# Modulation weight loads taken in pairs on four column tiles of 512 columns, with VectorE adding the partial sums

## The chip, the cores and the metric

The kernel runs on one core of one Trainium2 chip. Times are device microseconds (us) of that core from launch to end; three executions of the kernel before took 1745.45, 1746.52 and 1747.11 us, median 1746.52 us. The profile shows one further execution of the same program, taken by the hardware profiler.

## The reference

One step of one decoder layer for 256 prompt tokens and 8 sample tokens (264 columns), in float32. What matters here is the modulation: nine conditioning vectors (one for the prompt, eight for the samples) pass through a silu and a 2048 x 6144 weight matrix and give shift, scale and gate.

```python
def trunk_layer(x, c, prm, conv_prefix, h0, attend):
    mod = jax.nn.silu(c) @ prm['w_mod'] + prm['b_mod']
    shift, scale, gate = jnp.split(mod[:, None, :], 3, axis=-1)
    h = rmsnorm(x, prm['g_pre']) * (1 + scale) + shift
    (u_a, v_a, z_a, x_b, z_b, q, k, v, q_i, k_i, w_i, z_c, g_m) = split_proj(h @ prm['w_in'])
    ...
    merged = g[:, :, 0] * p_a + g[:, :, 1] * p_b + g[:, :, 2] * p_c
    o = merged @ prm['w_out']
    x = x + gate * rmsnorm(o, prm['g_post'])
```

## The kernel before

Activations stand with features on partitions and the 264 tokens along the free axis. A feature tile is 128 columns of a projection: 16 blocks of 128 x 128 weights, each multiplied three times (high by high, high by low, low by high part of a float32 split in two), so 48 matmuls of 264 columns for a tile. Weights come in **units** of eight blocks, 512 KB each, one DMA on SyncE's queue per unit; ScalarE makes the high part `wh` (line 302) and VectorE the low part `wl` (line 306), each in two halves of 512 columns, one to three units ahead of the product.

The modulation weights `w_mod` come over the same queue and into the same buffers (`raw`, six of them, and four extra `rawx` until the last load of shift and scale), again 512 KB for each load. They aren't split: `mod_item` (line 397) multiplies them in plain float32, with the nine vectors (`cpad`, padded to 32 columns) as the stationary operand, so that each matmul takes a tile of 128 rows by 32 columns of TensorE and four such column tiles can work at a time. `w_mod` is cut into pieces (`PIECES`, line 48): shift and scale of 1, 1, 2, 4, 4 and 4 blocks of features, then the gate in two halves. Pieces 0 and 1 have 4 loads each (four k each), piece 2 has 8 (two k each), pieces 3 to 5 and the two gate halves 16 each (one k of 1024 columns): 96 loads. In a load, `groups_of` gives each column tile its own quarter of the columns (128 or 256 of them, two tiles alone in pieces 0 and 1), and PSUM sums over k.

`_stream` (line 75) writes down the order in which loads are issued and used. The first 32 tiles (`EARLY`) are computed in parts of K: with the first piece of h they do one block each, and so on, while the next piece's modulation loads are put between their units; partial products are collected in SBUF (`part`, lines 1014 to 1022) by VectorE, in the first part by ScalarE too. The gate's 32 loads are put one behind each unit of the tiles `u` and `za`, in the middle of the kernel. TensorE works strictly in this order, so a modulation load stands between the matmuls of two units.

When a piece's last load has been used, `mod_piece` (line 450) copies the sums from PSUM (`ms`, line 440, on ScalarE), turns them by TensorE transposes (`modT`, line 434), adds the bias on VectorE and makes h's high and low parts `hh` and `hl`, which the next parts of the early tiles wait for. `mod_gate` (line 477) does the first half of that for the gate. The work of a piece is spread over the following products by `Tasks`.

## Time and profile before

| what | value |
|---|---|
| time, median of three executions | 1746.52 us |
| profiled execution: first to last instruction (span) | 1614.2 us |
| outside the span, by the median | 132.3 us |
| TensorE busy | 1578.5 us, 98% |
| VectorE busy | 990.1 us, 61% |
| ScalarE busy | 807.9 us, 50% |
| mean granted TensorE clock | 0.990 of full speed |
| data moved | 326.26 MB, mean 202 GB/s |

The trace holds the span alone; of the profiled execution's time outside it, nothing is recorded, so the 132.3 us are the difference to the median of the other three executions. A matmul in the trace is shown with its start and a modelled end: neighbours overlap, and the pace of TensorE is read from one start to the next. A float32 matmul leaves two records, so a load of 1024 columns with four matmuls shows as x8.

### The profile page before, as it was taken

What the parts mean: (1) busy time and instruction counts of PE and PEld (TensorE: products, weight loads), DVE (VectorE), ACT (ScalarE), POOL (GpSimd) and SP (SyncE); (2) the same over time, 40 slices, a digit from 0 to 9 for tenths busy, and PEclk for the clock granted to TensorE, in tenths of its full rate; (3) what the DMA queues carried; (4) which work ended last, traced back from release to release, by engine and by line L of the source; (5) the groups of instructions that cost most, each with busy time, mean ns of one, the idle gap of its engine ahead of it and who ended that gap; (6) DMA issues with size and microseconds to landing.
All of it is one profiled execution on the core that took longest, in us unless ns stands there. A gap on an engine that the chain in (4) does not pass through costs nothing.

```text
span 1614.2 us, 33342 instructions
## 1 busy us (share of the span) xinstructions
PE 1578.5 (98%) x13289; PEld 1518.1 (94%) x13289; DVE 990.1 (61%) x2111; ACT 807.9 (50%) x1628; POOL 295.5 (18%) x411
## 2 busy tenths in 40 slices
PE   8999999998889999999999999999999999999998
PEld 7888899998879999998889999999999999999997
DVE  6876589754446645544546654444777777766654
ACT  5333368554435444443334444444777777754442
POOL 4000256577730001000000000000211111100011
PEclk9999999999989999999999999999999999999999
DMA  8898863655445555657885556555465545555652
GB/s 337 304 362 286 284 207 119 192 180 155 156 151 174 185 182 184 201 184 268 286 273 186 172 182 235 181 181 181 152 198 174 173 162 186 180 190 183 234 183 83
DMA packets 91867, 326.26 MB, mean 202 GB/s; under 512 B 12320, under 2 KB 12768, under 8 KB 91328
## 3 DMA queue, kind: packets, MB, share of 16 engines
q1 hardware_dynamic: 86608, 313.18, 57.4%
q0 software_dynamic: 5104, 10.96, 2.3%
q8 instruction: 104, 1.70, 0.4%
q14 instruction: 51, 0.42, 0.1%
HBM read 320.35 MB, written 3.67 MB: 201 GB/s over the span
## 4 chain that ended last, share of the span: by engine, by line
PE 70%; DVE 1%; issue 0%; POOL 0%; DMA 0%; ACT 0%; DVEq 0%; ACTq 0%
PE acc L1010 68%; PE pmod L407 1%; PE spP L838 0%; PE giP L879 0%; PE gaP L879 0%; POOL gv L716 0%; DVE x L161 0%; DVE ls L158 0%; DMA gv<-in_cv,rows 0%; DVE ls L981 0%; DVE wl L160 0%; PE rsP L1063 0%; DVE o L158 0%; DVEq L1154 0%; ACT wh L157 0%
## 5 line engine op out<-in xcount | busy, mean ns | idle before, releaser
L160 DVE TENSOR_TENSOR wl<-raw,wh 128x512 fp32r<-128x512 f32 x926 | 613.2, 706 | 371.9 <-ACT wh L157 352.8
L1010 PE MATMUL acc<-hh,wh 128*128 128x264 f32 x2832 | 822.5, 290 | 6.8 <-DVE part L159 2.6
L1010 PE MATMUL acc<-hh,wl 128*128 128x264 f32 x2832 | 805.1, 284 | 1.9 <-DVE wl L160 1.9
L1010 PE MATMUL acc<-hl,wh 128*128 128x264 f32 x2832 | 806.0, 285 | 0.1
L157 ACT ACTIVATE wh<-raw 128x512 fp32r<-128x512 f32 x926 | 530.3, 622 | 496.6 <-PE acc L1010 357.4
L1010 PEld LDWEIGHTS acc<-hh,wh 128*128 128x128 f32 x2832 | 536.6, 189 | 41.0 <-issue 25.1
L1010 PEld LDWEIGHTS acc<-hl,wh 128*128 128x128 f32 x2832 | 537.0, 190 | 0.7 <-DVE hl L160 0.4
L1010 PEld LDWEIGHTS acc<-hh,wl 128*128 128x128 f32 x2832 | 534.2, 189 | 2.3 <-DVE wl L160 2.3
L1010 PE MATMUL acc<-ah,wh 128*128 128x264 f32 x768 | 217.9, 284 | 0.0
L1010 PE MATMUL acc<-al,wh 128*128 128x264 f32 x768 | 217.6, 283 | 0.0
L1010 PE MATMUL acc<-ah,wl 128*128 128x264 f32 x768 | 217.4, 283 | 0.0
L1010 PEld LDWEIGHTS acc<-al,wh 128*128 128x128 f32 x768 | 144.7, 188 | 0.0
L1010 PEld LDWEIGHTS acc<-ah,wh 128*128 128x128 f32 x768 | 144.6, 188 | 0.0
L1010 PEld LDWEIGHTS acc<-ah,wl 128*128 128x128 f32 x768 | 144.0, 187 | 0.0
L810 POOL TENSOR_TENSOR mg<-mg,gp 128x264 f32<-128x264 f32 x16 | 12.0, 752 | 473.8 <-DVE gp L161 473.8
L159 DVE TENSOR_TENSOR part<-acc,part 128x264 f32<-128x264 f32 x128 | 51.6, 428 | 35.6 <-PE acc L1010 35.2
L1010 PE MATMUL acc<-mh,wh 128*128 128x264 f32 x256 | 72.6, 284 | 0.0
L1010 PE MATMUL acc<-ml,wh 128*128 128x264 f32 x256 | 72.5, 283 | 0.0
L1010 PE MATMUL acc<-mh,wl 128*128 128x264 f32 x256 | 72.5, 283 | 0.0
L716 POOL DMA_INDIRECT gk<-in_ck,rows x64 | 64.2, 1003 | 19.4 <-issue 16.3
L716 POOL DMA_INDIRECT gv<-in_cv,rows x64 | 62.1, 970 | 19.5 <-issue 18.3
L1010 PEld LDWEIGHTS acc<-ml,wh 128*128 128x128 f32 x256 | 48.2, 188 | 0.0
(377 smaller groups left out, 1266.8 us busy)
## 6 DMA issues: line engine op xcount, KB each, us to landing
raw<-in_wall SPq DMA_DIRECT2D x463, 512.0 KB, 3.7
raw<-in_wmod SPq DMA_DIRECT2D x73, 512.0 KB, 5.6
rawx<-in_wmod SPq DMA_DIRECT2D x23, 512.0 KB, 6.4
rawx<-in_wall SPq DMA_DIRECT2D x19, 512.0 KB, 6.0
xr<-in_xT SPq DMA_DIRECT2D x4, 528.0 KB, 5.6
wrg<-in_wrg SPq DMA_DIRECT2D x1, 2048.0 KB, 8.5
x<-in_xp SPq DMA_DIRECT2D x1, 2048.0 KB, 9.5
out_yp<-x SPq DMA_DIRECT2D x8, 256.0 KB, 2.4
```

The lines of the kernel that those rows point to most:

```text
L157: copy = lambda out, x, scale=1.0: act.activation(out, x, AF.Copy, scale=scale)
L159: add = lambda out, x, y: dve.tensor_tensor(out, x, y, OP.add)
L160: sub = lambda out, x, y: dve.tensor_tensor(out, x, y, OP.subtract)
L407: pe.matmul(MOD[q][32 * g:32 * g + 32, 0:n], cpad[:, k, :], r[:, c:c + n], start=k == 0, stop=k == KB - 1, skip_group_check=True)
L716: pool.indirect_dma_start(out=to, out_offset=None, in_=a["ck" if what == "gk" else "cv"], in_offset=bass.IndirectOffsetOnAxis(ap=rows[:, n ...
L810: pool.tensor_tensor(S["mg"][:, j, :], S["mg"][:, j, :], x, OP.add)
L1010: pe.matmul(c[:, 0:T], x[:, kk * P:(kk + 1) * P], y[:, k, :], start=n == 0 and (kk == 0 if early else k == 0), stop=n == 2 and (kk == nk - ...
```

## The change

The 96 loads stay as they are, in size and content. What changes:

- `_stream` puts them in twos: two loads in a row, then units. The gate's pairs stand behind each whole tile (two units) and no longer one behind each unit.
- `mod_item` does nothing at a pair's first load and works off both at the second. The work of both is one list of (k, up to 512 columns), and entry x goes to column tile x mod 4. So a column tile no longer owns a part of the columns; it sums the k that fall to it, over 512 columns (256 in pieces 0 and 1).
- The copy out of PSUM takes two instructions where there are 512 columns, the first 256 columns on ScalarE, the others on VectorE; there are n / 128 transposes, and `tensor_reduce` on VectorE adds the partial sums over the column tiles into `mr`, from which the bias is added.

```diff
 def _stream():
             while done < len(ms) and done * MOD_BY <= j * len(ms):
-                items.append(ms[done])
-                done += 1
+                items += ms[done:done + 2]
+                done += 2
...
             items.append(("w", n, [(j, k0, 8)]))
             n += 1
-            if gate and ORDER[j][0] in ("u", "za"):
-                items.append(gate.pop(0))
+        if gate and ORDER[j][0] in ("u", "za"):
+            items += gate[:2]
+            del gate[:2]
...
-    def groups_of(q):
+    def shape_of(q):
         width = MODS[q][0][0]
-        groups = min(4, width // P)
-        return groups, width // groups
+        return width, min(512, width), max(1, width // 512)

     def mod_item(i):
         _, q, m = items[i]
-        width, ks, _ = MODS[q][m]
-        groups, n = groups_of(q)
-        if m == 0:
+        if m % 2 == 0:
+            return
+        width, n, halves = shape_of(q)
+        if m == 1:
             MOD[q] = pst("pmod")
-        r = used(i)
-        for x, k in enumerate(ks):
-            for g in range(groups):
-                c = x * width + g * n
-                pe.matmul(MOD[q][32 * g:32 * g + 32, 0:n], cpad[:, k, :], r[:, c:c + n],
-                          start=k == 0, stop=k == KB - 1, skip_group_check=True)
+        work = []
+        for x in (i - 1, i):
+            ks = MODS[q][items[x][2]][1]
+            r = used(x)
+            work += [(k, r[:, c * width + h * n:c * width + (h + 1) * n])
+                     for c, k in enumerate(ks) for h in range(halves)]
+        for x, (k, r) in enumerate(work):
+            g = x % 4
+            pe.matmul(MOD[q][32 * g:32 * g + 32, 0:n], cpad[:, k, :], r, start=m == 1 and x < 4,
+                      stop=m == len(MODS[q]) - 1 and x >= len(work) - 4, skip_group_check=True)
...
+    def mod_rows(q):
+        n = shape_of(q)[1]
+        p = MOD.pop(q)
+        ms = []
+        for c in range(0, n, 256):
+            ms.append(w("ms"))
+            (dve.tensor_copy if c else copy)(ms[-1][:, 0:256], p[:, c:c + 256])
+        return ms
+
     def mod_turn(q, ms):
-        groups, n = groups_of(q)
-        r = 32 * groups
+        _, n, halves = shape_of(q)
         pt = pss("modT")
-        for b in range(n // P):
-            pe.transpose(pt[:, b * P:b * P + r], ms[0:r, b * P:(b + 1) * P], ident[0:r, 0:r])
-        return pt[:, 0:n].rearrange("p (b g r) -> p b g r", b=n // P, g=4)
+        blocks = n // P
+        for b in range(blocks):
+            pe.transpose(pt[:, b * P:(b + 1) * P], ms[b // 2][:, b % 2 * P:(b % 2 + 1) * P], ident)
+        out = w("mr")[:, 0:halves * blocks * 9].rearrange("p (h b r) -> p h b r", h=halves, r=9)
+        for h in range(halves):
+            x = pt[:, 0:n].rearrange("p (b k h r) -> p h b r k", b=blocks, h=halves, r=32)
+            dve.tensor_reduce(out[:, h], x[:, h, :, 0:9, :], AX.X, OP.add)
+        return out.rearrange("p h b r -> p (h b) r")
...
     def mod_piece(q):
-        add(by_k(mB[:, ks, :], g), pt[:, :, 0:g, 0:9], by_k1(prm(C_BMOD, k0, nk), g))
-        add(by_k(mA[:, ks, :], g), pt[:, :, g:2 * g, 0:9], by_k1(bsc1[:, ks], g))
+        add(mB[:, ks, :], mr[:, 0:nk], each(prm(C_BMOD, k0, nk)))
+        add(mA[:, ks, :], mr[:, nk:2 * nk], each(bsc1[:, ks]))
```

Three places show how the order moves. On TensorE, before, at the start of the program (`rsP` and `rbP` are the norm of x, `raw_178` to `raw_182` the first five modulation loads, `acc` the first product):

```order
L175 MATMUL warm<-ones 128x128 x40
L407 MATMUL pmod<-raw_178,cpad 32x128 x8
L333 MATMUL rsP<-ones,sqacc 128x1 x3
L407 MATMUL pmod<-raw_179,cpad 32x128 x8
L407 MATMUL pmod<-raw_180,cpad 32x128 x8
L407 MATMUL pmod<-raw_181,cpad 32x128 x8
L342 MATMUL rbP<-dg,ones 128x264
L434 MATMUL modT<-ident,ms 128x64
L407 MATMUL pmod<-raw_182,cpad 32x128 x8
L1010 MATMUL acc<-hh,wh 128x264
```

The same place now:

```order
L177 MATMUL warm<-ones 128x128 x40
L335 MATMUL rsP<-ones,sqacc 128x1 x3
L414 MATMUL pmod<-raw_178,cpad 32x256 x4
L414 MATMUL pmod<-raw_179,cpad 32x256 x4
L414 MATMUL pmod<-raw_180,cpad 32x256 x4
L414 MATMUL pmod<-raw_181,cpad 32x256 x4
L344 MATMUL rbP<-dg,ones 128x264
L451 MATMUL modT<-ident,ms 128x128 x2
L414 MATMUL pmod<-raw_182,cpad 32x256 x4
L414 MATMUL pmod<-raw_183,cpad 32x256 x4
L1020 MATMUL acc<-hh,wh 128x264
```

Half as many matmuls of twice the columns; the first load's work now stands behind the norm's sum, and a sixth load is worked off ahead of the first product. The loads on SyncE's queue at the same place, before (`in_wall` holds the tiles' weights, `in_wmod` the modulation's):

```order
L268 DMA raw_181<-in_wmod 128x1024
L268 DMA raw_182<-in_wmod 128x1024
L270 DMA raw_183<-in_wall 128x1024
L268 DMA rawx<-in_wmod 128x1024
L270 DMA rawx<-in_wall 128x1024
L268 DMA rawx<-in_wmod 128x1024
L270 DMA rawx<-in_wall 128x1024
```

And now:

```order
L270 DMA raw_181<-in_wmod 128x1024
L270 DMA raw_182<-in_wmod 128x1024
L270 DMA raw_183<-in_wmod 128x1024
L272 DMA rawx<-in_wall 128x1024 x2
L270 DMA rawx<-in_wmod 128x1024 x2
```

The first unit of weights is now the seventh load, not the sixth. On VectorE, around the end of piece 2's loads, before (`part` are the early tiles' partial sums):

```order
L159 TENSOR_TENSOR part_256<-acc,part_256 128x264 x8
L160 TENSOR_TENSOR wl<-rawx,wh 128x512 x2
L159 TENSOR_TENSOR part_256<-acc,part_256 128x264 x2
L159 TENSOR_TENSOR mB<-modT,par 128x18
L159 TENSOR_TENSOR mA<-modT,bsc_127 128x18
```

And now, with what each waits for:

```order
L161 TENSOR_TENSOR part_256<-acc,part_256 128x264 [waits PE_49]
L442 COPY ms<-pmod 128x256 [waits Activation_49]
L161 TENSOR_TENSOR part_256<-acc,part_256 128x264 [waits PE_49]
L455 TENSOR_REDUCE mr<-modT 128x36 [waits PE_49]
L161 TENSOR_TENSOR mB<-mr,par 128x18 [waits DVE_49]
L161 TENSOR_TENSOR mA<-mr,bsc_127 128x18
```

A copy and a reduction are new in VectorE's queue; the copy waits for ScalarE's copy of the other half. By the two streams, the 96 loads made 72 separate interruptions of the units before (piece 0: 1, piece 1: 4, piece 2: 4, piece 3: 7, pieces 4 and 5: 12 each, gate 32), and now make 45 (1, 2, 4, 6, 8, 8, 16).

## Rows read from the trace of the kernel before

**Rows 1.** The page: the span, and busy time, share and instructions of each engine.
```profile
span 1614.2 us, 33342 instructions
...
PE 1578.5 (98%) x13289; PEld 1518.1 (94%) x13289; DVE 990.1 (61%) x2111; ACT 807.9 (50%) x1628; POOL 295.5 (18%) x411
```

**Rows 2.** Waits of TensorE: who waited for whom, total us, times, longest.
```profile
PE soP L746 <- DMA gv<-in_cv,rows: 15.3, 8, 5.0
PE acc L1010 <- DVE part L159: 2.6, 5, 0.7
```

**Rows 3.** Timeline of TensorE, one load alone: start, length, operation, idle time before it.
```profile
185.04 0.28 PE L1010 MATMUL acc<-hh,wl 128*128 128x264 f32 x1
185.25 0.64 PE L407 MATMUL pmod<-rawx,cpad 128*32 128x256 f32 x8
185.82 0.39 PE L1010 MATMUL acc<-hh,wh 128*128 128x264 f32 x1
186.05 0.29 PE L1010 MATMUL acc<-hl,wh 128*128 128x264 f32 x1
186.17 0.29 PE L1010 MATMUL acc<-hh,wl 128*128 128x264 f32 x1
```

**Rows 4.** Timeline of TensorE, two loads of piece 5 in a row.
```profile
188.72 0.28 PE L1010 MATMUL acc<-hh,wl 128*128 128x264 f32 x1
188.93 1.07 PE L407 MATMUL pmod<-raw,cpad 128*32 128x256 f32 x16
189.93 0.39 PE L1010 MATMUL acc<-hh,wh 128*128 128x264 f32 x1
190.15 0.28 PE L1010 MATMUL acc<-hl,wh 128*128 128x264 f32 x1
```

**Rows 5.** Timeline of TensorE, the one matmul of 512 columns, in two records.
```profile
234.09 1.12 PE L552 MATMUL vsP<-rs,sel 8*128 8x512 f32 x2
235.14 0.39 PE L1010 MATMUL acc<-hh,wh 128*128 128x264 f32 x1
```

**Rows 6.** Timeline of TensorE, the transposes of piece 5.
```profile
200.27 0.38 PE L434 MATMUL modT<-ident,ms 128*128 128x128 f32 x2
200.41 0.37 PE L1010 MATMUL acc<-hh,wh 128*128 128x264 f32 x1
```

**Rows 7.** Stretches: busy time (instructions) of PE, PEld, DVE, ACT, POOL; clock, DMA share, GB/s.
```profile
19.00:29.00 10.00, 6.59 (x48) 5.47 (x46) 7.35 (x14) 4.78 (x12) 6.99 (x8) 0.83 1.03 408
...
44.00:62.00 18.00, 16.78 (x221) 15.05 (x216) 16.71 (x46) 7.08 (x15) 0.00 (x0) 1.00 0.81 287
62.00:93.00 31.00, 29.92 (x300) 24.53 (x300) 20.53 (x49) 7.22 (x14) 0.00 (x0) 1.00 0.94 341
...
725.00:850.00 125.00, 125.00 (x1092) 107.42 (x1092) 60.93 (x116) 47.94 (x94) 0.00 (x0) 1.00 0.80 275
```

**Rows 8.** Timeline of ScalarE at the start of the program.
```profile
19.85 1.15 ACT L157 ACTIVATE wh<-raw 128x512 fp32r<-128x512 f32 x2 [1.91 <-DMA raw<-in_wall]
```

**Rows 9.** Timeline of TensorE: first product; a load of piece 1; a late unit.
```profile
21.64 0.39 PE L1010 MATMUL acc<-hh,wh 128*128 128x264 f32 x1 [1.89 <-ACT hh L157]
...
28.45 1.07 PE L407 MATMUL pmod<-rawx,cpad 128*32 128x128 f32 x16
29.44 0.39 PE L1010 MATMUL acc<-hh,wh 128*128 128x264 f32 x1
...
85.81 0.36 PE L1010 MATMUL acc<-hh,wh 128*128 128x264 f32 x1 [0.72 <-DVE part L159]
```

**Rows 10.** Groups of VectorE by shape: operation, count, busy us, mean ns, idle before.
```profile
L547 DVE COPY vn<-vP 128x256 f32<-128x256 f32 x4 | 1.6, 408 | 0.0
...
L159 DVE TENSOR_TENSOR mB<-modT,par 128x18 f32<-128x18 f32 x1 | 0.2, 165 | 0.0
```

**Rows 11.** One unit in the gate's stretch: its DMA issue (SyncE's timeline), its split (ScalarE, VectorE).
```profile
759.61 0.42 SPq L270 DMA_DIRECT2D raw<-in_wall  x1
...
764.35 1.15 ACT L157 ACTIVATE wh<-raw 128x512 fp32r<-128x512 f32 x2 [3.17 <-DMA raw<-in_wall]
...
765.01 1.29 DVE L160 TENSOR_TENSOR wl<-raw,wh 128x512 fp32r<-128x512 f32 x2 [3.30 <-ACT wh L157]
```

**Rows 12.** The same unit's first product on TensorE.
```profile
771.45 0.39 PE L1010 MATMUL acc<-hh,wh 128*128 128x264 f32 x1
```

More of the change, by code (lines that the diff above doesn't have):

```diff
@@ L13 @@
 OP = mybir.AluOpType
+AX = mybir.AxisListType
 PSUM = bass.MemoryType.PSUM
@@ L427, in mod_item, with each @@
                 tasks.spawn(mod_gate(q - len(PIECES)), 1)
+    def mod_rows(q):
[6 more added lines that the diff above has]
+        return ms
     def mod_turn(q, ms):
-        groups, n = groups_of(q)
-        r = 32 * groups
+        _, n, halves = shape_of(q)
         pt = pss("modT")
-        for b in range(n // P):
-            pe.transpose(pt[:, b * P:b * P + r], ms[0:r, b * P:(b + 1) * P], ident[0:r, 0:r])
-        return pt[:, 0:n].rearrange("p (b g r) -> p b g r", b=n // P, g=4)
-    def mod_rows(q):
-        groups, n = groups_of(q)
-        ms = w("ms")
-        copy(ms[0:32 * groups, 0:n], MOD.pop(q)[0:32 * groups, 0:n])
-        return ms
-    def by_k(x, g):
-        return x.rearrange("p (g b) r -> p b g r", g=g)
-    def by_k1(x, g):
-        b = x.shape[1] // g
-        return x.rearrange("p (g b) -> p b g", g=g)[:, :, :, None].to_broadcast([P, b, g, 9])
+        blocks = n // P
[6 more added lines that the diff above has]
+        return out.rearrange("p h b r -> p (h b) r")
+    def each(x):
+        return x[:, :, None].to_broadcast([P, x.shape[1], 9])
     def mod_piece(q):
@@ L453, in mod_piece @@
         yield 1
-        pt = mod_turn(q, ms)
+        mr = mod_turn(q, ms)
         ks = slice(k0, k0 + nk)
-        g = groups_of(q)[0] // 2
-        add(by_k(mB[:, ks, :], g), pt[:, :, 0:g, 0:9], by_k1(prm(C_BMOD, k0, nk), g))
-        add(by_k(mA[:, ks, :], g), pt[:, :, g:2 * g, 0:9], by_k1(bsc1[:, ks], g))
-        mul(mA[:, ks, :], mA[:, ks, :], prm(C_GPRE, k0, nk)[:, :, None].to_broadcast([P, nk, 9]))
+        add(mB[:, ks, :], mr[:, 0:nk], each(prm(C_BMOD, k0, nk)))
+        add(mA[:, ks, :], mr[:, nk:2 * nk], each(bsc1[:, ks]))
+        mul(mA[:, ks, :], mA[:, ks, :], each(prm(C_GPRE, k0, nk)))
         hs, samples = {}, w("hsm")[:, 0:nk * NS].rearrange("p (k b) -> p k b", k=nk)
@@ L480, in mod_gate @@
         yield 1
-        pt = mod_turn(len(PIECES) + q, ms)
+        mr = mod_turn(len(PIECES) + q, ms)
         ks = slice(k0, k0 + nk)
-        add(by_k(mG[:, ks, :], 4), pt[:, :, :, 0:9], by_k1(prm(C_BMOD, 2 * KB + k0, nk), 4))
-        mul(mG[:, ks, :], mG[:, ks, :], prm(C_GPOST, k0, nk)[:, :, None].to_broadcast([P, nk, 9]))
+        add(mG[:, ks, :], mr, each(prm(C_BMOD, 2 * KB + k0, nk)))
+        mul(mG[:, ks, :], mG[:, ks, :], each(prm(C_GPOST, k0, nk)))
     def gather_kix():
```

## The prediction

> **What bounds the kernel now.** I read the page's busy times first: TensorE is busy for 1578.5 of 1614.2 us, VectorE for 61% and ScalarE for 50% [rows 1]. The waits of TensorE are small and mostly elsewhere: 15.3 us for gathered cache rows in the attention, which the change does not touch, and 2.6 us for VectorE's partial sums, near the start [rows 2]. So nearly everywhere a microsecond taken out of TensorE's order is a microsecond of the program, and the change has to be priced by what stands in that order. Then the table of stretches, to find where this does not hold: from 44 to 62 us VectorE is busy for 16.71 of 18.00 us, and from 62 to 93 us the DMA engines for 94%; in the gate's stretch, 725 to 850 us, TensorE is busy for all 125.00 us, VectorE for half, and DMA moves 275 GB/s of the 408 that it reached at the start [rows 7]. The sum is made on the span. The 132.3 us outside it (1746.52 less 1614.2) are not recorded; I take them as unchanged and set the sum against the median.
>
> **What an interruption costs.** The timeline shows one load between two units: from the last matmul before it to the second after it, 185.04 to 186.05, are 1.01 us, where two ordinary steps are 0.24 (186.05 to 186.17 is one of 0.12) [rows 3]. So a load alone costs 0.77 us. Two loads in a row: 188.72 to 190.15 are 1.43 us, less 0.24 is 1.19 [rows 4]. The second load thus adds 0.42, its columns, and 0.35 belong to the interruption: the first matmul begins 0.21 us after the one before it, and the two acc steps behind the load take longer. Two loads apart cost 1.54, as a pair 1.19: 0.35 us saved for each interruption that goes.
> The Trainium skill, page "TensorEngine Tiling (Array Packing)", Key Properties, says that changing the tiling mode drains TensorE; by that the price sits at entry and exit and not with the load, which the 0.42 of the second load agrees with. If it sat with the load, pairing would give nothing: that is the second rival below.
>
> **What 512 columns cost.** Before, a wide load is two rounds of 256 columns on four tiles at once. Now a pair is two rounds of 512. If a column keeps its price, that is 2 x 0.42 again, 1.19 us for a pair. The only matmul of 512 columns in the trace, alone on TensorE, takes 1.05 us from its first record to the next acc matmul (234.09 to 235.14), where the two loads of 256 columns take 1.00 (188.93 to 189.93) [rows 4, 5]. So a pair costs between 1.19 and 1.24; I take 1.19, since that matmul has another shape (8 rows) than the four tiles, and keep 0.05 x 44 pairs = 2.2 us for the upper end. In the other direction I see nothing: the columns per tile are the same.
>
> **The sum from piece 4 on**, where nothing but TensorE binds. The gate has 32 interruptions before and 16 now: 16 x 0.35 = 5.6 us less. Pieces 4 and 5 have 12 each before (eight single loads and four twos), 8 now: 8 x 0.35 = 2.8 us less. Each of these four pieces is turned by four transposes in place of two; two cost 0.14 us from the first to the acc matmul behind them [rows 6], so 4 x 0.14 = 0.6 us more. Net 7.8 us less. The new copies and reductions on VectorE lie beside TensorE's work here: a copy of 256 columns out of PSUM is 0.41 us, and a reduction of up to 144 elements per partition lies between 0.17 us (an addition of 18 elements) and that 0.41 [rows 10]; one copy and two reductions for a piece are at most 1.2 us, and nothing waits for them, since VectorE idles half of the gate's stretch, and the transposes stand at least a product of 2.9 us behind the copies. A pair also holds two buffers until its second load is used. In the gate's stretch a unit's DMA is issued at 759.61, ScalarE starts on it, just landed, at 764.35, VectorE ends at 766.30, and TensorE takes it at 771.45: 5.1 us to spare [rows 11, 12], which covers a buffer that comes free up to one unit (2.9 us) later. So I cost the pairs' hold at nothing.
>
> **The sum up to 93 us**, where TensorE is not alone. Four things, with both signs.
> First, the first unit of weights is now the seventh load. 512 KB at 408 GB/s are 1.29 us [rows 7], ScalarE waits for exactly this landing (19.85) [rows 8], and the first product waits for ScalarE (21.64, 1.89 us idle) [rows 9]: +1.3 us.
> Second, piece 1. Its loads have only two column tiles at work before: a load costs 0.99 us from first record to the next acc matmul (28.45 to 29.44), as much as two wide ones [rows 4, 9]. Now a pair does four loads' rounds in the time of two. Of the three interruptions of 1.2 us that stand behind the first product, one is left (the pair ahead of the first product falls into the wait for the weights): -2.4 us, if TensorE is what binds there. Piece 0 gets faster in the same way, but lies ahead of that wait: nothing.
> Third, from 44 to 62 us VectorE has 1.3 us of 18 left [rows 7], and it gets a copy and a reduction there (0.6 to 0.8 us). The copy waits in VectorE's queue for ScalarE's copy of the same PSUM tile, and behind it wait a partial sum and the `wl` of the next unit. The third of the four transposes waits for it, on TensorE, with the next matmuls behind: in piece 2 the transposes stand six matmuls (0.7 us) behind the last load, while ScalarE's and VectorE's copies take some 0.8 us in a row and a partial sum (0.4) lies ahead of the second. That is up to +0.5 us in each of pieces 2 and 3, and some of what piece 1 saved is lost to VectorE.
> The Trainium skill's page "VectorE: DVE Perf Modes", Rules for kernel authors, speaks against the reduction: `tensor_reduce` on the hot path is the slowest of VectorE's operations and should be restructured away. No row here shows one; at the 0.41 taken above as its top it would be 0.2 us dearer than at the bottom, once in this stretch, so the sum moves by less than the bounds.
> Fourth, in 62 to 93 us the DMA engines are at 94%, and at 85.81 TensorE idles 0.72 us at the start of a unit that has just come in [rows 7, 9]. The pairs put one more load ahead of that unit (16 of piece 3 and not 15): between nothing and +1.3 us. Piece 3 saves one interruption, 0.35, and pays 0.14 for transposes.
> Together the early part lies between -2.6 + 1.3 = -1.3 us (all of pieces 1 and 3 comes through, nothing else is late) and 1.3 + 0.6 + 1.0 + 1.3 = +4.2 (nothing comes through). I take +0.5: VectorE and DMA set the pace from 44 to 93 us, so most of piece 1's gain is stopped there, while part of the lateness is taken up by VectorE's slack between 20 and 44 us.
>
> **Forecast.** -7.8 + 0.5 = -7.3 us, 0.42%: 1746.5 - 7.3 = 1739.2 us. Chance 0.72; its own range is 1737 to 1742.
>
> **Rivals.**
> (1) The early part eats half: +4.2 us as above, so -3.6 and 1742.9 us. For it: VectorE at 93% and DMA at 94% one after the other. Against it: TensorE's waits of all kinds there are only a few us today. Chance 0.12.
> (2) The change doesn't do what it says: the extra time sits with the load, or 512 columns on four tiles at once cost more than twice 256, so that a pair costs 1.54 us again. Then -8.4 becomes 0, the transposes and the early part stay: +0.6 + 0.5, 1747.6 us. Against it: the 0.42 of the second load. Chance 0.06.
> (3) The early part gives something: -1.3 us, in all -9.1 and 1737.4, or somewhat more if piece 1's gain moves the DMA ahead as well, since buffers come free sooner. Chance 0.06.
> (4) Slower: the gate's weights come late. Two loads of w_mod now stand in the queue ahead of two units, and their buffers come free together. If a unit's landing is put off by the two loads ahead of it (2 x 1.29), the pair's own hold (1.2) and a unit's time (2.9), that is 6.7 us against 5.1 to spare [rows 11], 1.6 us of waiting for each of 16 pairs, 25 us, and 1746.5 - 7.3 + 25 = 1764 us; it passes the gain from a delay of 5.6 us on. For it: ScalarE takes the unit as soon as it lands, so there is no stock of landed weights. Against it: four loads in a pair's period of 7.0 us (two units and 1.2) are 2.1 MB, 300 GB/s of the 408 that were reached. Chance 0.04.
>
> **How the numbers follow.** About 0.2%, 3.5 us, is what a measurement of this kernel can tell from no change. The forecast and rival 3 are faster by more, and half of rival 1: 0.72 + 0.06 + 0.06 = 0.84. The other half of rival 1 and rival 2 are within it: 0.12. Rival 4 is slower: 0.04. The range of 8 in 10 goes from 1736.5 (rival 3 with some of the DMA gain) to 1743.0 (rival 1, which also takes in the forecast with the dearer 512 columns, 1741.4); rivals 2 and 4 and the edges are left out.
>
> **What would show it.** In the gate's stretch each pair stands in the timeline as two rounds of records, four at a time and some 0.43 us apart, and costs 1.19 us between units, 16 times; 1.4 or more speaks for rival 2. The first acc matmul starts at about 22.9 us and not 21.64. Early units' starts tell the second, third and fourth step: the unit that starts at 85.81 would start between 84.5 and 90, and a wait of TensorE for VectorE's `ms` copy would show at the transposes of pieces 2 and 3. From there to the end of piece 5 the gain should grow by 2.8 us less 0.3, and between 725 and 850 us by 5.3. Waits of TensorE on `wh` or `wl` between 725 and 850 us, none now, would show rival 4. The forecast is wrong if the gain at the end of the gate's stretch is under 3.5 us, or if the time outside the span moves.

## The result

The changed kernel is slower: 1756.11 us median (1755.15 to 1760.23, 4 runs) against 1746.82 us (1745.45 to 1749.71, 4 runs) of the kernel before, a ratio of 1.0057 with a 95% interval of 1.0043 to 1.0070. I had forecast 1739.2 us and a range up to 1743.0. So 9.3 us came where 7.3 were to go.

The page of the changed kernel, span and busy times, to be set against [rows 1]:

```profile
span 1754.2 us, 32431 instructions
...
PE 1601.8 (91%) x12824; PEld 1525.2 (87%) x12824; DVE 991.5 (57%) x2130; ACT 808.2 (46%) x1628; POOL 294.9 (17%) x411
```

140 us more than the span of [rows 1] cannot be the change, since the times differ by 9.3. A second profile of the kernel before (experiment before_again), from a chip on which it takes 1741.99 us, shows what it is. Its waits of TensorE (who waited for whom, total us, times, longest):

```profile
core 0 of [0], span 1742.0 us
...
PE acc L1010 <- issue: 60.6, 50, 2.4
PE spT L736 <- ACT oc L157: 27.2, 2, 14.3
PE sP L678 <- issue: 20.1, 1, 20.1
```

and the same view of the changed kernel, which answers to [rows 2]:

```profile
core 0 of [0], span 1754.2 us
...
PE acc L1020 <- issue: 66.3, 58, 2.5
PE spT L746 <- ACT oc L159: 23.9, 2, 12.3
PE sP L688 <- issue: 17.3, 1, 17.3
...
PE acc L1020 <- ACT wh L159: 6.5, 9, 1.1
PE acc L1020 <- DVE wl L162: 3.8, 11, 1.3
...
PE modT L451 <- DVE ms L442: 2.0, 4, 0.9
```

The first three lines are alike in both kernels, 107.9 and 107.5 us in sum; in two of them (`issue`) TensorE waits for nothing that the profile shows. None of the three is among the waits of the first profile [rows 2], whose largest was 15.3 us. That is a stop-and-go during GpSimd's gathers, and the profile that I forecast from is of an execution that had none of it (the last section). What the change brings is in the lower three: TensorE waits for the split weights `wh` and `wl` (in the second profile of before 0.7 us once and 1.8 us in two waits), and the transposes wait for VectorE's copy `ms` (not at all before). Against the second profile of before, the starts of the units on TensorE (start of a unit's first `acc` matmul in the timeline, us, numbered from 0) show where the 12.2 us between the two spans come from:

| stretch | before_again | changed | difference |
|---|---|---|---|
| start to unit 16 (pieces 0 to 3) | 97.1 | 100.7 | +3.6 |
| units 16 to 32 (loads of piece 4) | 58.2 | 56.9 | -1.3 |
| units 32 to 48 (loads of piece 5; the first gathers) | 71.6 | 67.9 | -3.7 |
| units 48 to 194 (no loads of `w_mod`; gathers) | 623.5 | 626.3 | +2.8 |
| units 194 to 260 (the gate's loads) | 223.5 | 234.3 | +10.8 |
| unit 260 to the end | 668.1 | 668.3 | +0.1 |

The third and fourth line also hold the stop-and-go, which varies by some us from one execution to the next. What is left is a loss of 10.8 us in the gate's stretch, where I had forecast a gain of 5.3, and one of 3.6 us in the early part, where I had +0.5.

**The gate's stretch.** It starts at 850 us here. The stretches of the changed kernel (busy time and instructions of PE, PEld, DVE, ACT and POOL; clock, DMA share, GB/s), which answer to the last of [rows 7]:

```profile
850.00:900.00 50.00, 50.00 (x406) 44.12 (x405) 22.22 (x42) 17.30 (x33) 0.00 (x0) 1.00 0.65 230
900.00:990.00 90.00, 80.83 (x605) 66.13 (x605) 40.07 (x79) 28.64 (x59) 0.00 (x0) 1.00 0.66 240
```

and of before in its second profile:

```profile
850.00:900.00 50.00, 50.00 (x439) 42.87 (x438) 24.36 (x46) 20.35 (x38) 0.00 (x0) 1.00 0.77 260
900.00:979.00 79.00, 79.00 (x690) 68.55 (x689) 39.12 (x76) 29.77 (x60) 0.00 (x0) 1.00 0.81 282
```

For 50 us both are without a wait, and from unit 194 to unit 208 the changed kernel takes 50.8 us, 1.8 less than before: the pairs' gain comes through. But it already moves less data, 230 and not 260 GB/s, so it lives on weights that came in earlier. Then TensorE is idle for 9 of 90 us, at 240 GB/s. The DMA engines are less busy than before (0.66 and 0.81), so they are not the limit; something issues too late. The timeline of one period shows what, first SyncE's issues, then ScalarE's and VectorE's split of units 206, 207 and 208, then TensorE (start, length, engine, operation, idle time before it):

```profile
895.27 0.80 SPq L270 DMA_DIRECT2D raw<-in_wmod  x2
896.12 2.03 SPq L272 DMA_DIRECT2D raw<-in_wall  x2
903.84 0.80 SPq L270 DMA_DIRECT2D raw<-in_wmod  x2
...
893.29 1.15 ACT L159 ACTIVATE wh<-raw 128x512 fp32r<-128x512 f32 x2 [4.26 <-DMA raw<-in_wall]
...
895.85 1.15 ACT L159 ACTIVATE wh<-raw 128x512 fp32r<-128x512 f32 x2 [1.13 <-DMA raw<-in_wall]
901.85 1.15 ACT L159 ACTIVATE wh<-raw 128x512 fp32r<-128x512 f32 x2 [4.85 <-DMA raw<-in_wall]
...
893.95 1.29 DVE L162 TENSOR_TENSOR wl<-raw,wh 128x512 fp32r<-128x512 f32 x2 [4.12 <-ACT wh L159]
...
893.69 0.28 PE L1020 MATMUL acc<-hh,wl 128*128 128x264 f32 x1
893.90 1.06 PE L414 MATMUL pmod<-raw,cpad 128*32 128x512 f32 x8
894.90 0.39 PE L1020 MATMUL acc<-hh,wh 128*128 128x264 f32 x1
895.13 0.28 PE L1020 MATMUL acc<-hl,wh 128*128 128x264 f32 x1
...
902.53 0.39 PE L1020 MATMUL acc<-hh,wh 128*128 128x264 f32 x1 [0.57 <-ACT wh L159]
```

The pair itself is as forecast: 893.69 to 895.13 are 1.44 us, less two ordinary steps (0.24) 1.20, where I had 1.19. But read the issues. SyncE issues nothing until 895.27, just after the split of unit 206 ends at 895.24 (893.95 + 1.29). In the rotation of buffers, the next load of `w_mod` is to go where unit 206 stood. SyncE works in order, so the second load and unit 208 wait behind it, though their two buffers, those of the pair ahead of unit 204, had been free since that unit started at 887.47. The third issue, at 896.12, is unit 208; it lands at 901.85 behind the two loads, and only then its own split can begin, at whose end the next pair may be issued. That closes a loop: split 1.95 us (893.29 to 895.24), issues 0.88, landing 5.73, together 8.56 us for a period in which TensorE has work for 7.2 (two units of 2.9, a pair, and a few matmuls of what follows the tiles; the mean of the sixteen periods of mod_first, which have no wait). From 901.85 on the periods are 8.3 and 9.2 us.

The kernel before has this loop too, with one load in it. The unit of [rows 11] is issued at 759.61 and its split ends at 766.30; then SyncE issues a load and, behind it, the unit after next:

```profile
766.33 0.33 SPq L268 DMA_DIRECT2D raw<-in_wmod  x1
766.71 0.43 SPq L270 DMA_DIRECT2D raw<-in_wall  x1
```

From 759.61 to 766.71 are 7.10 us, while TensorE had work for 7.56 us in two units and their two loads (121.0 us for units 194 to 226). So the loop was shorter than the work by half a us, and a late landing could be made up: the turn from 762.12 took 8.77 us, the next one 6.92. The pairs put two loads ahead of the unit in place of one; the loop is 1.5 us longer by these two turns, and the work 0.3 us shorter.

**The early part.** The first product starts 0.5 us later than before [rows 9]. Units 1 to 7 start up to 1.5 us earlier than in the second profile of before (and at most 0.5 us earlier than in the first), units 8 to 12 within 0.4 us, and the loss comes at units 13 to 16. One pair of traces does not give its size: five traces of this study with the early part of the kernel before (before, before_again, gate_only, gate_order, paced_kix) start unit 16 at 97.0 to 98.2 us, seven with the changed one (after, pieces_only, pieces_again, mod_first, more1, gate_spread, kix_paced) at 99.0 to 101.2, a difference of 2.9 us between the means. The timeline of the changed kernel there, VectorE, then TensorE:

```profile
89.57 0.42 DVE L161 TENSOR_TENSOR part<-acc,part 128x264 f32<-128x264 f32 x1
89.91 0.41 DVE L442 COPY ms<-pmod 128x256 f32<-128x256 f32 x1
90.25 0.42 DVE L161 TENSOR_TENSOR part<-acc,part 128x264 f32<-128x264 f32 x1
90.86 0.37 DVE L455 TENSOR_REDUCE mr<-modT 128x36 f32<-128x72 f32 x2 [0.19 <-PE modT L451]
...
87.58 0.36 PE L1020 MATMUL acc<-hh,wh 128*128 128x264 f32 x1 [1.85 <-DVE part L161]
...
89.11 0.38 PE L451 MATMUL modT<-ident,ms 128*128 128x128 f32 x2
90.38 0.44 PE L451 MATMUL modT<-ident,ms 128*128 128x128 f32 x2 [0.89 <-DVE ms L442]
90.57 0.37 PE L1020 MATMUL acc<-hh,wh 128*128 128x264 f32 x1
```

Unit 13 starts at 87.58 after 1.85 us of idle time, where [rows 9] had 0.72 at 85.81: the last load of piece 3 now goes out ahead of it and not behind it. So the turn of piece 3 falls into this unit, 1.5 us after its start. The third and fourth transposes wait for VectorE's copy, which stands behind a split and a partial sum in VectorE's queue. From 89.11 to 90.57 TensorE does four transposes that take 0.14 us for two [rows 6].

### The profile page after: what moved, and what is told of

The parts are those of the page before. It is cut to its first block, busy times and chain, and to the rows that moved or that the text cites. A ratio compares the mean times of both kernels' runs of the same rounds, so it can differ in the third digit from the quotient of the medians.

```text
span 1754.2 us, 32431 instructions
## 1 busy us (share of the span) xinstructions
PE 1601.8 (91%) x12824; PEld 1525.2 (87%) x12824; DVE 991.5 (57%) x2130; ACT 808.2 (46%) x1628; POOL 294.9 (17%) x411
## 4 chain that ended last, share of the span: by engine, by line
PE 80%; issue 7%; DVE 5%; DMA 5%; ACT 2%; another core or an unknown queue 2%; SPq 0%; DVEq 0%; ACTq 0%
PE acc L1020 75%; DMA raw<-in_wall 3%; DVE wl L162 2%; PE pmod L414 2%; ACT wh L159 1%; DMA rawx<-in_wall 1%; DVE part L161 1%; DMA xr<-in_xT 0%; PE oP L701 0%; PE giP L889 0%; PE gaP L889 0%; PE sP L689 0%; PE spP L848 0%; SPq L270 0%
## 5 line engine op out<-in xcount | busy, mean ns | idle before, releaser
L1020 PEld LDWEIGHTS acc<-hh,wh 128*128 128x128 f32 x2832 | 543.1, 192 | 82.5 <-issue 38.3
L1020 PEld LDWEIGHTS acc<-hl,wh 128*128 128x128 f32 x2832 | 543.2, 192 | 28.0 <-issue 27.3
L1020 PEld LDWEIGHTS acc<-hh,wl 128*128 128x128 f32 x2832 | 540.8, 191 | 29.2 <-issue 23.0
L683 DVE COPY qpad<-qt 128x4 f32<-128x4 f32 x32 | 4.0, 179 | 96.0 <-ACT qt L159 62.6
```

What stands on the lines that cost most here:

```text
L683: dve.tensor_copy(qpad[n % 2][:, :, 36 * s + hh4], qs[:, :, s])
L1020: pe.matmul(c[:, 0:T], x[:, kk * P:(kk + 1) * P], y[:, k, :], start=n == 0 and (kk == 0 if early else k == 0), stop=n == 2 and (kk == nk - ...
```

## The experiments

The first four ran on one chip, which took 1741.99 us for the kernel before (11 runs), the next four on one that took 1618.46 us (19 runs) and shows no stop-and-go; the four after them on one that took 1741.76 us (17 runs). The last three are single executions on a fourth, where one of the kernel before took 1738.45 us.

**before_again.** The kernel before, unchanged.

> The kernel before, unchanged, for one more profile. Theory A (the first profile of before, 1614.2 us against a median of 1746.8, is an execution without the idle time of all engines that the profile after shows between 300 and 560 us, and the timed executions of before have it too): a span near 1745 us, over 80 us of TensorE's idle time put down to issue between 200 and 560 us, and the units 210 to 227 (gate's stretch) in 63.7 us as in the first profile. Rival B (the 132 us lie outside the span in before, and the idle time is new with the change): a span of 1614 us again.

1743.71 us, with a span of 1742.0 us. So only 1.7 us lie outside the span, and nearly all of the 132.3 us that I took for unrecorded time were stop-and-go that the first profile lacked.

**pieces_only and gate_only.** Each has half of the change. Written with flags:

```diff
+PAIR_PIECES, PAIR_GATE = True, False     # pieces_only; gate_only: False, True
-                items += ms[done:done + 2]
-                done += 2
+                items += ms[done:done + (2 if PAIR_PIECES else 1)]
+                done += 2 if PAIR_PIECES else 1
```

> Pairs for the pieces of shift and scale alone; the gate's loads stand one behind each unit and are worked off as before. Theory A (the loss is in the gate's stretch: the loads behind a pair get their buffers late and weights land late): the time of before plus what the early part shows in the two profiles, 0.9 us: 1747 to 1749 us, and the gate's stretch (units 210 to 227) at 63.7 us. Rival B (the loss is in the attention, which the changed early part shifts against the cache gathers): 1754 to 1757 us.

> Pairs for the gate alone; the early pieces as before. Theory A: all of the loss, 1746.8 + 8 to 11 = 1755 to 1758 us, with 74 us for the units 210 to 227 and waits of TensorE for ScalarE's wh there. Rival B (loss in the attention): the gate's saving of the forecast comes through, 1746.8 - 5.3 = 1741.5 us.

pieces_only took 1731.03 us (ratio 0.9928, interval 0.9915 to 0.9940) and gate_only 1752.61 us (1.0059, 1.0046 to 1.0072). Units 194 to 235 take 148.4 us in pieces_only, as before, and 160.6 in gate_only: the gate carries the loss. pieces_only fits neither of the two times that I expected. The 11 us that pieces_only gains are not what its pairs save. At unit 16 it stands at 101.0 us, 3.9 behind before_again; between units 32 and 48 it takes 55.4 us and not 71.6, without stop-and-go (below, pieces_again).

**gate_order.** The gate's loads in twos in the stream, but each worked off alone, in 256 columns on each column tile, as before.

```diff
-            if gate and ORDER[j][0] in ("u", "za"):
-                items.append(gate.pop(0))
+        if gate and ORDER[j][0] in ("u", "za"):
+            items += gate[:2]
+            del gate[:2]
```

> The kernel before, in which the gate's loads stand in twos behind each tile, but each is worked off by itself on four column tiles of 256 columns, and the early pieces are as before. Theory A (it is the place in the stream, which sets when buffers come free and loads start): slow as gate_only, 1755 to 1758 us. Rival C (it is the work of a pair, 512 columns or two buffers held to the end): 0.35 us saved for each of 16 interruptions, 1741 us.

1754.42 us (1.0082, 1.0067 to 1.0098); units 194 to 235 take 159.2 us, as in the changed kernel (159.1). So the order in which the loads stand costs all of it, and working off as a pair costs nothing that shows.

**mod_first.** The changed kernel, with two rules on buffers: what a load of the gate gives back goes to the next load in line, and nothing is issued at the turn of a pair's second load, so that the buffer of the unit just split is left for a unit.

```diff
     def used(i):
-        free.append(RAW.pop(i))
-        return free[-1][0]
+        x = RAW.pop(i)
+        if items[i][0] == "m" and items[i][1] >= len(PIECES):
+            free.insert(0, x)
+        else:
+            free.append(x)
+        return x[0]
...
-        while room(loaded):
+        second = it[0] == "m" and it[1] >= len(PIECES) and it[2] % 2 == 1
+        while not second and room(loaded):
```

**more1** keeps the changed kernel's rotation and gives it a seventh buffer for loads (two small work buffers fewer, to make room). **gate_spread** keeps the rotation and the six buffers, and puts one pair behind every fourth unit.

```diff
-        if gate and ORDER[j][0] in ("u", "za"):
+        if gate and ORDER[j][0] in ("u",):        # gate_spread
...
+        free.append((ab.tile([P, 8 * P], F32, name="rawm"), True))   # more1, ahead of the gate's stretch
```

> The changed kernel; only which buffer a load takes is different in the gate's stretch: the two buffers of a pair go to the next two modulation loads, and the buffer of a weight unit to a weight unit. Theory A (the loop behind the loss is: a unit lands, is split in 2.0 us, only then the next pair's first load gets that unit's buffer, and the next unit stands behind both loads in the queue, 5.7 us from issue to landing, 8.6 us in all where TensorE needs 7.0): the two loads start when the pair is done, the loop falls to about 7 us, and units 194 to 235 go from 159 us to 143 to 147; the whole 12 to 16 us under the changed kernel, so between 6 us under and 0 us over the kernel before of the same chip. Rival D (six buffers are too few whichever takes which): 155 us or more for units 194 to 235.

> The changed kernel with a seventh buffer for loads from the tiles pc on (and ten work tiles in place of twelve, to make room). Theory A: four loads in 8.6 us with six buffers become four in about 7.3 us with seven: units 194 to 235 in 143 to 149 us in place of 159, 10 to 16 us under the changed kernel. Rival E (the loss comes from the order of ScalarE's or VectorE's work, not from the loads): 157 to 160 us.

> The changed kernel, with the gate's pairs behind the tiles u alone, so one pair for four units over the whole stretch of u and za. Theory A: six loads in 12.8 us of TensorE's time, well under what the loop gives; no waits for wh, all 16 interruptions saved: units 194 to 260 (which hold all of the gate's loads here and before) take 5 us less than the 223.5 us of before, 218 us, and 17 us less than the changed kernel. Rival E: the pairs themselves hold things up: 16 waits as in the changed kernel.

mod_first took 1614.09 us (0.9972, 0.9962 to 0.9983), more1 1615.15 (0.9983, 0.9974 to 0.9992) and gate_spread 1613.74 (0.9971, 0.9959 to 0.9983): each of the three is faster than before by 3 to 5 us and faster than the changed kernel on this chip (1629.02, kix_paced below) by 14 to 15, and each breaks the loop in another way. Units 194 to 235 take 143.3 us in the first two, where the sum of my prediction gives 143.1 (148.4 less 5.3); units 194 to 260 take 218.4 us in gate_spread, and 223.5 less 5.3 is 218.2. SyncE's issues of mod_first in the gate's stretch, and its stretches:

```profile
788.96 0.81 SPq L275 DMA_DIRECT2D raw<-in_wmod  x2
791.25 4.13 SPq L277 DMA_DIRECT2D raw<-in_wall  x2
796.84 0.80 SPq L275 DMA_DIRECT2D raw<-in_wmod  x2
```

```profile
724.00:774.00 50.00, 50.00 (x408) 43.54 (x406) 24.65 (x47) 20.14 (x38) 0.00 (x0) 1.00 0.83 270
774.00:850.00 76.00, 76.00 (x619) 66.78 (x612) 40.40 (x80) 30.44 (x62) 0.00 (x0) 1.00 0.87 289
```

The loads now go out at the end of a pair (TensorE begins one at 787.83 and one at 795.71, 1.06 us each), the units at the end of a split; both still stand in one queue, but no load of `w_mod` waits for a split. TensorE has no wait in the stretch, at 289 GB/s: the data could come faster than the 240 of the changed kernel.

**kix_paced.** The changed kernel, with the 16 gathers of `kix` written down two to a product, so that other work stands between them.

```diff
+                if i % 2:
+                    yield 1        # inside the loop over the gathers
```

> The changed kernel; the 16 gathers of the indexer's keys are issued two behind each product and no longer all in a row. The kernel with pairs for the pieces alone passed units 45 to 60 in 60 us, the kernel before and the changed one lose 13 us there, while GpSimd issues these gathers one every 1.25 us and all engines show idle time put down to issue. Theory F (a long unbroken run of gathers holds up the instructions of all engines): the 13 us go, 1742 to 1744 us against 1754 to 1756 of the changed kernel. Rival G (the hold-up doesn't depend on the run of gathers): no change, 1754 to 1756 us.

Nothing makes GpSimd wait, so it ran the 16 in a row all the same, and the pacing was not tried by this. The run is a repeat of the changed kernel on a chip without stop-and-go: 1629.02 us (1.0068, 1.0055 to 1.0082), +10.6 us, and 158.0 us for units 194 to 235.

**late_pieces, pieces_again and best.** late_pieces pairs pieces 4 and 5 alone; pieces_again is pieces_only once more; best has the pairs of pieces 4 and 5, those of the gate, and mod_first's rules.

```diff
+PAIR_PIECES, PAIR_GATE = 4, False     # late_pieces; best: 4, True
-        return PAIR_PIECES if q < len(PIECES) else PAIR_GATE
+        return q >= PAIR_PIECES if q < len(PIECES) else PAIR_GATE
```

> Only pieces 4 and 5 of shift and scale are worked off in pairs; pieces 0 to 3 and the gate stand as before. My theory (an interruption less is 0.35 us less wherever nothing but TensorE binds): eight interruptions fewer, less four more transposes, 2.5 us less than before; the starts of the units up to the twentieth stand where they stand before, within 0.5 us. The rival (the early part's loss comes from reductions and copies of any paired piece): no change, or up to 1 us more. Where the stop-and-go of the index gathers behind unit 45 shows in before and not here, another 13 us less come from that alone, and the units' starts ahead of it decide.

> All six pieces in pairs, the gate as before, as was run already. If the 11 us that it gained there came from the stop-and-go of the index gathers alone (13.6 us between units 45 and 48), then on a chip where before shows none it is 1 to 3 us slower than before, and the stretch from unit 45 to 48 is the same in both. If the pairs of the pieces themselves gained, it is 8 to 12 us faster again.

> Pieces 4 and 5 and the gate in pairs, pieces 0 to 3 as before, and a buffer of the gate's loads is given to the gate's next load, so that a unit never waits for it. If the loss of the changed kernel sits in two places alone (early pieces, and the gate's buffers), both are gone here: 2.5 us less for pieces 4 and 5 and 5.1 us less for the gate, 7 to 8 us less than before, about what I had forecast for the whole change. If the gain of pieces 4 and 5 isn't there, 4 to 5.5 us less.

late_pieces took 1740.91 us (0.9993, 0.9984 to 1.0002), which is not to be told from before, where I expected 2.5 us less; units 16 to 32 took 57.0 us, 1.2 less than before, and units 32 to 48 69.0, 2.5 less, stop-and-go included. pieces_again, with a median of 1730.68 us (0.9942, 0.9924 to 0.9961), tells what the 11 us are: of its six executions four took 1728.8 to 1731.1 us and two 1739.2 and 1742.3, and one of those two was profiled. It takes 67.6 us for units 32 to 48, where pieces_only took 55.4. Stretches of pieces_only and of pieces_again around the gathers of `kix`:

```profile
185.00:225.00 40.00, 40.00 (x327) 37.89 (x326) 28.60 (x68) 18.71 (x38) 20.73 (x20) 1.00 0.69 227
```

```profile
185.00:225.00 40.00, 32.82 (x228) 29.36 (x228) 21.46 (x50) 11.66 (x22) 16.66 (x16) 0.83 0.53 174
```

The same program does 327 matmuls in one execution and 228 in another. So the gain comes and goes with the stop-and-go, and it isn't time that the pairs save. Nine of the eleven executions of this kernel on two chips took less than 1733 us, and none of the 28 of the kernel before there less than 1738; why the pairs escape it so often is not shown, and on a chip without it pieces_only was not run.

best took 1732.27 us (0.9946, 0.9934 to 0.9959), 9.5 us less than before, in five executions within 2.3 us. By its trace against before_again, the start of unit 16 is 0.6 us later, units 16 to 32 take 1.2 us less, and units 194 to 260 take 218.4 us, 5.1 less, without a wait; the rest of the 12.6 us between their spans lies in stretches with stop-and-go. The pairs' own share is thus 1.2, some 1.5 for piece 5 (units 32 to 48 took 56.9 us in [rows 1]'s execution and 55.4 in mod_first, neither with stop-and-go) and 5.1, together 7.8 us: what I had forecast for everything from piece 4 on. Of the kernels with pairs it is the fastest on chips with stop-and-go, but for those executions in which the pairs of all pieces escaped it. It was not run on the chip without.

**paced_kix.** The kernel before, with GpSimd made to wait, ahead of every second gather of `kix`, for a memset that VectorE does at that unit.

```diff
+    def pace(i):
+        if i % 2 == 0:
+            dve.memset(tok[0:1, 0:1], 0.0)
+            pool.tensor_copy(tok[0:1, 1:2], tok[0:1, 0:1])
```

> The kernel before, with the 16 index gathers that GpSimd issues in a row held to two for each unit: ahead of each two, GpSimd waits for a small memset that VectorE does at that unit. Theory (a long row of gathers issued back to back is what stops and starts all engines behind unit 45): on a chip that shows it in before, the stretch from unit 45 to 48 falls from about 24 to about 9 us, so 12 to 14 us less; on a chip that doesn't, no change within 1 us. Rival (it has another cause, and only falls into the same stretch): no change on either.

1734.63 us (0.9954, 0.9940 to 0.9968), 7.1 us less, about half of what I expected. Units 32 to 60 took 113.0 us, where before_again took 122.5 and the first profile of before, without stop-and-go, 107.9. So the pace of the gathers has a part in it, and the rival (no change) falls; but two gathers to a unit are still one in 1.46 us, and some of the stop-and-go stayed.

**only_p01, only_p2 and only_p3.** One piece in pairs and all else as before, to see which of the four early steps costs the 3.6 us: `paired(q)` holds for 0 and 1, for 2, or for 3.

> Only pieces 0 and 1 are worked off in pairs. If the seventh load ahead of the first unit costs anything by unit 16, it shows here: my steps one and two give +1.3 and -2.4 us, of which by the changed kernel's records little is left, so unit 16 starts within 0.5 us of before (97.0 to 98.2). The rival (the lateness of the first unit is handed on through the DMA queue) puts it 1 to 3 us later.

> Only piece 2 in pairs (its loads stand among units 4 to 7). By my third step its added VectorE copy and reduction cost up to 0.5 us at unit 8; unit 16 within 0.7 us of before (97.0 to 98.2). The rival (VectorE, with 1.3 us of slack in 18, hands all of the copies on): 1 us and more later from unit 8 on.

> Only piece 3 in pairs (its loads stand among units 8 to 15). My fourth step taken at its upper end, and the transposes that wait for the second copy: unit 13 lands later by a load, and unit 16 starts 2 to 3.5 us later than before, so that nearly all of the early loss is here. If the loss is the sum of small parts of all pieces, 1 us or less.

| start of unit, us | 0 | 4 | 7 | 8 | 12 | 13 | 14 | 16 |
|---|---|---|---|---|---|---|---|---|
| before_again | 21.6 | 44.8 | 58.4 | 63.4 | 81.1 | 86.0 | 89.8 | 97.1 |
| paced_kix (early part as before) | 21.8 | 44.7 | 58.4 | 63.4 | 81.1 | 87.7 | 91.3 | 98.2 |
| only_p01 | 22.9 | 44.9 | 58.5 | 63.5 | 81.2 | 87.0 | 90.6 | 97.5 |
| only_p2 | 21.9 | 45.5 | 58.3 | 64.2 | 82.0 | 87.8 | 91.4 | 98.3 |
| only_p3 | 21.8 | 44.5 | 58.2 | 63.4 | 80.6 | 88.2 | 93.5 | 101.2 |

The executions took 1742.54, 1741.70 and 1745.07 us; single times on a chip with stop-and-go say little here, the starts of the units more. Kernels that are alike up to unit 16 differ by 1.1 us there, so only only_p3 stands out: piece 3 carries most of the early loss. only_p2 shows a smaller one, 0.8 us at unit 8 where I expected up to 0.5. From unit 7 to unit 8, where the turn of piece 2 falls, it takes 5.95 us and before_again 5.02: the transposes wait 0.27 us for `ms`, and TensorE's wait for a partial sum of VectorE's ends 4.19 us after the unit's start (62.47) and not 3.25 (61.64). The changed kernel takes 6.11 us for this unit, in all seven traces that have its early part, and loses there the lead of 1.1 us that it had at unit 7. only_p3's waits of TensorE from 62 to 104 us:

```profile
PE acc L1070 <- ACT wh L164: 2.5, 1, 2.5
PE acc L1070 <- DVE part L166: 0.4, 1, 0.4
PE modT L466 <- DVE ms L486: 0.3, 1, 0.3
```

The order of events is that of the changed kernel: the unit behind the last load is late, and the turn falls into it. The clock fell here as well (the last section).

## Why the prediction was wrong, step by step

**What an interruption costs** and **what 512 columns cost** held. A pair takes 1.20 us (forecast 1.19), and where nothing but TensorE binds, the gate's pairs give 5.1 us (5.3 with the transposes), piece 4's 1.3 and piece 5's 1.5 (1.25 each). My rival (2), that the change does not do what it says, falls with it.

**"So I cost the pairs' hold at nothing"** is the step that failed, by 16 us (+10.8 for -5.3). I took the 5.1 us between a unit's landing and its use [rows 11, 12] as a reserve that a later landing may use up once. That a buffer comes free one unit later was counted; that the next load in SyncE's queue gets the buffer of a unit just split, with units waiting behind it for buffers that are free, was not. The delay is then not subtracted from a reserve but handed on: each landing sets the split that sets the next issue. The reserve lasted to about 900 us, and from there on each period was late. Such a loop has to be added up link by link, and its length (8.56 us, 7.10 before) set against the work that it feeds (7.2, 7.56 before). My rival (4) had the right place and the right signs, a unit behind two loads and a pair that holds; with 25 us its price was too high (units 194 to 235 take 15.8 us more than without waits, 159.1 against 143.3), as it charged a wait to each of 16 pairs and left out the reserve, and its chance of 0.04 rested on GB/s, which are a bound only where issues are not late. mod_first, more1 and gate_spread show the loop from three sides, and gate_order shows that it comes from the order of the loads and not from the work of a pair.

**The early part** came out at +3.6 us by the changed kernel's trace, 2.9 by the means of all traces, where I took +0.5, inside the bounds of -1.3 and +4.2 that I gave. Step one was sized too high: the first product starts at 22.08 to 22.86 us in the eight traces with six loads ahead of the first unit and at 21.07 to 21.90 in the nine others, 0.6 later by the means and not 1.3, and by unit 4 it is taken up. Step two's 2.4 us are there in part (units 1 to 7 start up to 1.5 us earlier) and gone at unit 8, as I had said of most of it, since VectorE sets the pace up to 62 us [rows 7]. Step three has the mechanism, but was sized too low: in piece 2 the unit with the turn is 0.9 us longer (only_p2), as the partial sum that TensorE waits for comes that much later in the unit, and in piece 3 the transposes wait 0.89 us, not 0.5. Step four, the unit behind the sixteenth load, is seen at unit 13: 1.85 us idle and not 0.72. What I did not see is that steps three and four meet: as the last load goes ahead of unit 13, the turn moves into that unit too.
The Trainium skill's page "VectorE: DVE Perf Modes", Rules for kernel authors, which I had set against the reduction, is neither borne out nor refuted here, since no run takes the reduction out: two reductions take 0.37 us together in piece 3, less than one at my upper end.

**The 132.3 us outside the span** were a wrong reading. As both kernels have the stop-and-go where the times were taken, the difference that I forecast was not touched by it, but some us of scatter in the stretches with gathers are.

## What to carry over

A buffer rotation with loads of two kinds has one queue in order: before loads are moved together, write down for each issue which release it waits for, follow that back to the landing that it started from, and set the length of the loop against the work that a turn of it feeds, in the kernel before as well: how much is left there is how much longer the loop may become. Slack between landing and use is a stock that a longer loop empties, and a DMA rate below the peak does not show that loads can come sooner. Where the profiled execution's span and the median differ by 130 us, profile once more before a stretch is read off it.

## What was not expected of the hardware

**Stop-and-go during gathers.** On every chip of this study but the one with 1618.46 us, TensorE, ScalarE and VectorE all go on by single instructions while GpSimd issues its indirect gathers back to back. GpSimd, then TensorE, in before_again:

```profile
203.42 0.94 POOL L491 DMA_INDIRECT kix<-in_cidx,rows  x1 [0.30 <-issue]
204.67 0.94 POOL L491 DMA_INDIRECT kix<-in_cidx,rows  x1 [0.30 <-issue]
205.92 0.94 POOL L491 DMA_INDIRECT kix<-in_cidx,rows  x1 [0.30 <-issue]
...
203.88 0.57 PE L1010 MATMUL acc<-hl,wh 128*128 128x264 f32 x1 [0.34 <-issue]
205.28 0.38 PE L1010 MATMUL acc<-hh,wl 128*128 128x264 f32 x1 [0.84 <-issue]
206.68 0.38 PE L1010 MATMUL acc<-hh,wh 128*128 128x264 f32 x1 [1.02 <-issue]
```

and a stretch of the same kernel further on, with gathers of the attention's cached keys and values (`gk`, `gv`):

```profile
325.00:403.00 78.00, 16.69 (x47) 12.65 (x47) 7.53 (x26) 3.95 (x10) 51.01 (x53) 0.50 0.19 53
```

A gather is issued every 1.25 us, and TensorE does a matmul in 1.40 us that otherwise starts every 0.12. From 325 to 403 us TensorE is busy for 16.69 of 78 us, and the granted clock is 0.50, its lower level. The whole costs 128 us between the two profiles of the kernel before (1742.0 and 1614.2). That it comes with the gathers is shown by their times and by paced_kix; why it comes on one chip or in one execution and not in another is not settled. The pace alone is not enough: pieces_only issues its first gathers of `kix` 1.25 us apart as well, and TensorE doesn't stop there. Nor is it shown where the first profile of before belongs; its span and clock (1614.2 us, 0.990) are like those of the kernel before on the chip without stop-and-go (1613.3 to 1618.8 us, 0.988 to 0.992).

**The clock falls in small gaps too.** In only_p3 TensorE waited 2.54 us ahead of unit 13, and then its granted clock fell to the lower level for some 3 us. Its stretches, the wait at the end of the first:

```profile
84.50:88.00 3.50, 1.17 (x12) 0.21 (x6) 1.57 (x4) 2.09 (x4) 0.00 (x0) 1.00 0.91 370
...
89.30:92.60 3.30, 3.02 (x15) 2.62 (x14) 2.80 (x10) 0.00 (x0) 0.00 (x0) 0.50 0.89 338
```

Matmuls start 0.22 us apart there and not 0.12. In mod_first, which has the changed kernel's early part, TensorE waited 2.1 us at the same place, and the clock fell as well (0.51 from 89.30 to 92.60 us); in the changed kernel (1.85 us) and in pieces_only (2.0) it stayed at full speed. Unit 16 started at 101.2 us in only_p3 and mod_first, and at 100.7 and 101.0 in the other two, so little of what the clock cost shows at unit 16.
